# Layer 1's value projection by 512 columns: four pairs of heads in one job, with another order of filling work

## The chip, the cores and the metric

The kernel runs on one core of one Trainium2 chip. The metric is the device time of one execution in microseconds (us); lower is better. Before the change it is 1191.08 us, the median of 3 runs (1190.09 to 1192.74). One further execution was profiled: it took 1189.34 us, and its span from the first to the last instruction is 1187.6 us.

Engines are named as in the profile: PE (matrix products), PEld (its weight loads), DVE, ACT and POOL (elementwise work), and SP, whose in-order queue issues every DMA.

## The reference, cut to what matters

A trunk of two residual layers over 1024 tokens of width 1024, in float32. Layer 0 mixes a differential attention with a bidirectional linear recurrence; layer 1, which the change concerns, is a neighbourhood attention with 16 heads of 64:

```python
h = rms_norm(x, norm_g[l]) * (1.0 + scale[:, None, :]) + shift[:, None, :]
...
proj = h @ w_in                                    # (1024, 1024) @ (1024, 4096)
q, k, v, g = jnp.split(proj, 4, axis=-1)
out = neighborhood_attention(q, k, v, rpb)         # 8 x 16 window, softmax, @ v
y = (out * jax.nn.silu(g)) @ w_out
x = x + gate[:, None, :] * y
```

## The kernel before, in words

**Products in three parts.** Every large product is made of three (`mm3`, L202): both operands are split into a rounded part (`hi`) and a rest (`lo`), and hi x hi, hi x lo and lo x hi are summed in one PSUM bank. In the profile these are the lines L204, L205 and L206.

**Weights come as slabs.** The weights are cut into 80 slabs of 512 KB. `load_next` (L152) issues one slab's DMA on SP into one of two `raw` buffers. `split_next` (L161) turns it into a `hi` tile on ACT (L187) and a `lo` tile on POOL (L188); only then is the raw buffer free for the slab after next. The tiles `whi` and `wlo` have two buffers in the pool `wp`, and a third in layer 1 (`state["third"]`). `slab(i)` makes sure that slab i is split; `ahead(i)` splits it early.

**Layer 1.** The activations are split once and stay (`hact`, names `ahi` and `alo`). Of its slabs a key, query or gate slab holds 128 output columns, and `proj` (L233) multiplies it in two halves of 24 products of 512 tokens each. The value slabs go the other way round, since the attention wants tokens on the partitions: `v1_job(p)` (L1232) takes two slabs, 256 output columns, which are two pairs of heads, and for each of 8 blocks of 128 tokens it makes 24 products, with the token block as the weights and 256 columns of the slabs as the moving side. There are four such jobs (p = 0, 2, 4, 6). Each block's result is copied from PSUM into a tile `vt` (two buffers) by DVE (L1250) or ACT (L1248), in turn, and stored to DRAM (`vd`); `load_v` (L1257) reads it back in the shape that the attention wants.

**The attention** runs over 64 units (8 pairs of heads, each with 8 blocks of 128 queries) in a pipeline. `na_a(u)` makes four logit products (L667, L668), DVE adds the bias (L1351), ACT takes the exponential (L1354), and POOL normalises (L1359); `na_b(u)` transposes on PE (L1370, tiles `etr`) and copies back; `na_c` multiplies four units by the values (L1388). On PE the order is: transposes of unit u, logits of unit u + 2, some filling work, transposes of unit u + 1, and so on.

**The filling work** is layer 1's own projection, in a queue of jobs (`Feed`, L54). After each `na_a` the loop calls `feed.pump(PUMP1)`: jobs are advanced, at a price of 1300 for each step of 6 products of 512 columns or 12 of 256, until the credit of 4400 is used up (6600 for the first three units). `feed.upto(name)` runs a job to its end where the attention needs it. The first key, query and gate (slabs 40, 41, 42) are multiplied before the attention starts; the first value job's slabs are 43 and 44, and the key of pair 1 is slab 45.

**Places in SBUF.** The eight tiles `mix0` to `mix7` hold the attention's gated outputs, and are empty until these come. Slab 42 (the first gate) is already split into `mix6` and `mix7`.

**The second layer's modulation** (`mod_part`, tiles `ada`, `macc`) is accumulated on DVE, one step after each unit from unit 26 on.

A scheduler places the instructions of every engine in a fixed order; at run time each engine works through its own in that order and waits where an input is missing. SP's DMA issues wait in the same manner, so what stands behind a waiting issue waits too.

Of the kernel before, what the change touches and what calls it, by code (L numbers as in the profile page):

```python
# [11 lines left out]
F32 = mybir.dt.float32  # L12
# [7 lines left out]
P = 128  # L20
# [77 lines left out]
def kernel(ctx, tc, xT, xTp, small, lamp, adaw, tb, w0, gw, wo0, w1, nab, wo1, out):  # L98
# [62 lines left out]
    def split_next():  # L161
        i = state["split"]
        if i >= len(slabs):
            return
        while state["load"] <= i:
            load_next()
        raw = raws.pop(i)
        pool = wp
        if state["third"] is not None:
            state["turn"] = (state["turn"] + 1) % 3  # L170
            pool = wp if state["turn"] else state["third"]
        tags = ("whi", "wlo")
        if i == 2:
            pool, tags = kqp, ("ks1", "ks1")
        if i == at1["g", 0]:
            pool, tags = mixp[1], ("mix6", "mix7")
        j = i - len(slabs) + KC
        if j >= 0:

            pool = (wp, kqp, mixa, mixp[1])[j // 2]  # L180
            if j >= 2:
                tags = (("ks0", "ks0"), ("ks1", "ks1"), ("mix0", "mix1"), ("mix2", "mix3"),
                        ("mix4", "mix5"), ("mix6", "mix7"))[j - 2]
        hi = pool.tile([P, KC, P], F32R, tag=tags[0], name=f"whi{i}")
        lo = pool.tile([P, KC, P], F32R, tag=tags[1], name=f"wlo{i}")
        with tc.high_priority() if j < 2 else tc.issue_after(state["pool"]):
            A.activation(hi[:], raw[:], AF.Copy)  # L187
            G.tensor_tensor(lo[:], raw[:], hi[:], ALU.subtract)  # L188
# [260 lines left out]
    for p in range(NA_PAIRS):  # L449
        vs = [("v", p), ("v", p + 1)] if p % 2 == 0 else []  # L450
        kq = [("k", p), ("q", p)]
        order1 += kq + vs if p else kq + [("g", 0)] + vs
        if 0 < p < LATE:
            order1.append(("g", p))
    order1 += [("g", p) for p in range(LATE, NA_PAIRS)]
    base1 = {"q": 0, "k": 8, "v": 16, "g": 24}
    for key in order1:
        at1[key] = len(slabs)
# [726 lines left out]
    with tc.tile_pool(name="bound", bufs=2) as bp:  # L1185
# [36 lines left out]
    with ExitStack() as l1:  # L1222
# [9 lines left out]
        def v1_job(p):  # L1232

            i = at1["v", p]
            ws = [slab(i), slab(i + 1)]
            for t in range(8):
                hf, b = divmod(t, 4)
                ps = bank("v1")
                for k in range(KC):
                    hi, lo = (t[:, b * P:(b + 1) * P] for t in hact[k, hf])  # L1240
                    wh, wl = (w[:].rearrange("p (k a) n -> p k (a n)", a=2)[:, k % 4, :]
                              for w in ws[k // 4])
                    mm3(ps[:, :256], hi, lo, wh, wl, k == 0, k == KC - 1)
                    if k == 3:
                        yield 1300.0
                vt = ap.tile([P, 256], F32, tag="vt", name="vt", bufs=2)
                if t % 2:
                    A.activation(vt[:], ps[:, :256], AF.Copy)  # L1248
                else:
                    V.tensor_copy(vt[:], ps[:, :256])  # L1250
                state["vd"] = nc.sync.dma_start(
                    vd4[2 * hf:2 * hf + 2, 64 * b:64 * b + 64, P * p:P * p + 256], vt[:]).ins
                if t == 1:
                    ahead(i + 2)
                yield 1300.0

        def load_v(p, b):  # L1257
# [9 lines left out]

        def load_ahead(p):

            if f"1v{p + 1 - (p + 1) % 2}" in feed.done:  # L1270
                for b in range(4):
                    load_v(p + 1, b)

# [14 lines left out]

        state["gate1"] = gate1
        feed.done.add("1g0")  # L1290
        for p in range(NA_PAIRS):
            if p:
                feed.add(f"1k{p}", both(at1["k", p], evac_k(("b", p))))
                feed.add(f"1q{p}", both(at1["q", p], evac_q(("b", p))))
            if p % 2 == 0:
                feed.add(f"1v{p}", v1_job(p))
            if 0 < p < LATE:
                feed.add(f"1g{p}", both(at1["g", p], evac_g1l(p)))
        for p in range(LATE, NA_PAIRS - 2):
            feed.add(f"1g{p}", both(at1["g", p], evac_g1l(p)))  # L1300

        def last_gates():

# [101 lines left out]
        es, ets = {0: na_a(0)}, {}  # L1405
        for u in range(n_units + 1):

            pump = 1.5 * PUMP1 if u < 3 else PUMP1
            if u and u % 4 == 0:
                na_c(u - 4, [ets.pop(u - 4 + b) for b in range(4)])  # L1410
            if u % 8 == 2:

                p = u // 8
                feed.upto(f"1v{p - p % 2}")
                for b in range(4):
                    load_v(p, b)
            elif u >= 8:
# [51 lines left out]

def _slabs_v(w):  # L1470

    n = w.shape[1] // 256
    return w.reshape(2, 4, P, n, 256).transpose(3, 0, 2, 1, 4).reshape(2 * n, P, KC, P)


def _t5_bucket(rel):
# [75 lines left out]
```

## Time and profile before

| | |
|---|---|
| time, median of 3 runs | 1191.08 us (1190.09 to 1192.74) |
| time of the profiled execution | 1189.34 us |
| span of the profiled execution | 1187.6 us |
| PE busy | 1141.8 us, 96% of the span |
| DVE, ACT, POOL busy | 62%, 47%, 31% |
| products of the value jobs, 256 columns | 768 |
| chain of work that ended last | PE 74%, DVE 13%, ACT 5% |

How to read it: a matrix product's own duration in the profile holds its passage through the array, and the next product starts before it ends. What a row of products costs is therefore read from the starts in the timeline: last start less first start, divided by the number of intervals. "Granted clock" is the share of full speed that PE was given.

### The profile page before, as it was taken

How to read it: one execution, taken by the hardware profiler on the slowest of the kernel's cores; microseconds unless marked ns; L12 is line 12 of the kernel's file. 1: busy time of each engine (PE TensorE's matmuls, PEld its weight loads, DVE VectorE, ACT ScalarE, POOL GpSimd, SP SyncE). 2: the span in 40 equal slices, each digit the busy share in tenths (PEclk: the TensorE clock that was granted, in tenths of full speed). 3: DMA queues.
4: the chain of work that ended last, by engine and by line, in shares of the span. 5: the costliest groups of instructions: out<-in, count | busy, mean ns of one | idle time of the engine just before them, and what ended most of it. 6: DMA issues, size and time to landing. Idle time of an engine off the chain costs nothing.

```text
span 1187.6 us, 19215 instructions
## 1 busy us (share of the span) xinstructions
PE 1141.8 (96%) x7232; PEld 972.4 (82%) x7232; DVE 735.3 (62%) x1422; ACT 564.0 (47%) x1029; POOL 372.2 (31%) x346
## 2 busy tenths in 40 slices
PE   5999889999999999999999999999999999999997
PEld 3788768788887888777878888988998998888896
DVE  6757957689899989878663344233434443555354
ACT  4457486565655556523442444344444434445121
POOL 2124321233333322344422433332333333316100
PEclk9999999999999999999999999999999999999999
DMA  9723122423123112476513433243453534314212
GB/s 329 237 73 126 49 95 80 144 65 94 28 70 105 31 41 72 133 243 235 182 48 123 139 112 89 89 133 105 132 174 88 159 128 119 92 36 155 99 72 71
DMA packets 85789, 136.46 MB, mean 115 GB/s; under 512 B 8000, under 2 KB 49472, under 8 KB 85696
## 3 DMA queue, kind: packets, MB, share of 16 engines
q1 hardware_dynamic: 85696, 135.23, 36.7%
q8 instruction: 57, 0.93, 0.3%
q14 instruction: 36, 0.29, 0.1%
HBM read 112.13 MB, written 16.78 MB: 109 GB/s over the span
## 4 chain that ended last, share of the span: by engine, by line
PE 74%; DVE 13%; ACT 5%; DMA 3%; issue 2%; POOL 2%; SPq 0%; DVEq 0%; ACTq 0%; POOLq 0%
PE pp L204 14%; PE pp L205 14%; PE pp L206 14%; PE no L1388 4%; PE etr L1370 3%; PE v L204 2%; PE v L206 2%; PE v L205 2%; PE n L667 2%; PE atr L1003 2%; DVE e L973 2%; PE n L668 2%; POOL wlo L188 1%; PE s L667 1%; PE s L668 1%
## 5 line engine op out<-in xcount | busy, mean ns | idle before, releaser
L204 PE MATMUL pp<-ahi,whi 128*128 128x512 f32 (+1 forms) x976 | 370.2, 379 | 1.0 <-DVE sgb L673 1.0
L206 PE MATMUL pp<-ahi,wlo 128*128 128x512 f32 (+1 forms) x976 | 367.7, 377 | 1.1 <-POOL wlo L188 1.1
L205 PE MATMUL pp<-alo,whi 128*128 128x512 f32 (+1 forms) x976 | 368.1, 377 | 0.0
L188 POOL TENSOR_TENSOR wlo<-raw,whi 128x1024 fp32r<-128x1024 f32 x80 | 197.0, 2465 | 267.4 <-ACT whi L187 245.3
L206 PEld LDWEIGHTS pp<-ahi,wlo 128*128 128x128 f32 x976 | 183.8, 188 | 35.4 <-POOL wlo L188 1.6
L204 PEld LDWEIGHTS pp<-ahi,whi 128*128 128x128 f32 x976 | 183.8, 188 | 34.0 <-DVE sgb L673 1.7
L205 PEld LDWEIGHTS pp<-alo,whi 128*128 128x128 f32 x976 | 183.8, 188 | 30.4
L1359 POOL TENSOR_SCALAR e<-e,r 128x288 f32<-128x288 f32 (+1 forms) x128 | 71.1, 568 | 234.7 <-DVE r L1357 234.3
L187 ACT ACTIVATE whi<-raw 128x1024 fp32r<-128x1024 f32 x80 | 84.2, 1055 | 98.7 <-PE pp L205 52.8
L977 ACT ACTIVATE e<-e,nm 128x1024 f32<-128x1024 f32 x64 | 73.6, 1151 | 46.3 <-DVE nm L973 46.0
L1354 ACT ACTIVATE e<-e,nm 128x288 f32<-128x288 f32 (+1 forms) x128 | 72.7, 569 | 46.1 <-DVE nm L1351 39.2
L1376 DVE COPY e<-etr 96x384 f32<-96x384 f32 (+1 forms) x64 | 35.5, 554 | 95.2 <-PE etr L1370 93.5
L1351 DVE CUSTOM_DVE_ANT_0 e<-n,bias 128x288 f32<-128x288 f32 (+1 forms) x128 | 60.6, 504 | 46.8 <-PE n L668 33.0
L1374 ACT ACTIVATE e<-etr 96x384 f32<-96x384 f32 (+1 forms) x64 | 31.3, 489 | 118.3 <-DVE e L1376 118.0
L973 DVE CUSTOM_DVE_ANT_0 e<-s,tb 128x1024 f32<-128x1024 f32 x64 | 77.3, 1218 | 6.0 <-PE s L668 4.3
L994 POOL TENSOR_SCALAR e<-e,r 128x256 f32<-128x256 f32 x32 | 32.6, 1018 | 130.9 <-DVE r L983 80.7
L204 PE MATMUL v<-whi,ahi 128*128 128x256 f32 x256 | 72.2, 282 | 0.0
L206 PE MATMUL v<-whi,alo 128*128 128x256 f32 x256 | 71.9, 281 | 0.0
L205 PE MATMUL v<-wlo,ahi 128*128 128x256 f32 x256 | 71.9, 281 | 0.0
L1010 ACT ACTIVATE ath<-atr 128x512 fp32r<-128x512 f32 x64 | 37.5, 596 | 38.1 <-PE atr L1003 37.8
L1370 PE MATMUL etr<-ident,e 128*96 128x128 f32 (+1 forms) x384 | 52.5, 272 | 2.0 <-POOL e L1359 2.0
L667 PE MATMUL s<-ks,qq 128*128 128x512 f32 x128 | 52.4, 409 | 0.0
(218 smaller groups left out, 2107.7 us busy)
## 6 DMA issues: line engine op xcount, KB each, us to landing
raw<-in_w_dram SPq DMA_DIRECT2D x56, 512.0 KB
ada<-in_adaw_dram SPq DMA_DIRECT2D x96, 256.0 KB
raw<-in_wo_dram SPq DMA_DIRECT2D x24, 512.0 KB
bias<-in_nab_dram SPq DMA_DIRECT2D x64, 144.0 KB
qq<-qq SPq DMA_DIRECT2D x48, 128.0 KB
bias<-in_nab_dram SPq DMA_DIRECT2D x32, 192.0 KB
xT<-in_xT_dram SPq DMA_DIRECT2D x16, 256.0 KB
vd<-vt SPq DMA_DIRECT2D x32, 128.0 KB
```

The costliest lines, as they stand in the source:

```text
L187: A.activation(hi[:], raw[:], AF.Copy)
L188: G.tensor_tensor(lo[:], raw[:], hi[:], ALU.subtract)
L204: T.matmul(ps, lh, rh, start=start, stop=False)
L205: T.matmul(ps, lh, rl, start=False, stop=False)
L206: state["pe"] = T.matmul(ps, ll, rh, start=False, stop=stop).ins
L667: T.matmul(dst, qsel(q[m]), k, start=True, stop=False)
L973: state["dve"] = V.tensor_tensor_reduce(out=e[:], in0=ps[:].rearrange("p a b -> p (a b)"), in1=tbt["tb"][:, o:o + S], scale=-1.0, scalar=3 ...
L977: A.activation(e[:], e[:], AF.Exp, scale=-1.0, bias=nm[:], accum_out=sums[:, m:m + 1])
L1351: state["dve"] = V.tensor_tensor_reduce(out=e[:, m, :n], in0=ps[:, m, :n], in1=bias["now"][m][:, :n], scale=-1.0, scalar=3.0e38, op0=ALU.a ...
L1354: A.activation(e[:, m, :n], e[:, m, :n], AF.Exp, scale=-1.0, bias=nm[:, m:m + 1], accum_out=sums[:, m:m + 1])
L1359: state["pool"] = G.tensor_scalar(e[:, m, :n], e[:, m, :n], r[:, m:m + 1], 0.0, ALU.mult, ALU.add).ins
L1370: T.transpose(pt[:kn, m, j * P:(j + 1) * P], e[:, m, j * kn:(j + 1) * kn], ident[:])
```

## The change

One value job now makes four pairs of heads: it takes four slabs at once, and each product has 512 moving columns, so there are two jobs (p = 0 and p = 4) of 8 x 24 products in place of four of 8 x 24 products of half the width. The host lays the value slabs out accordingly: each holds two of the eight blocks of the contraction for 512 columns. The chain of 24 products starts with the third and fourth slab. The result of a token block is copied out in two halves, one by DVE and one by ACT, into the same two buffers `vt`, and stored by two DMAs.

The third and the fourth slab of a job are split into places of later outputs: `mix4`/`mix5` and `mix2`/`mix3` for the first job, `mix4`/`mix5` and `mix6`/`mix7` for the second. All four slabs of the first job are asked for before the attention starts.

The order of the jobs is written as a string. The credit is 5000 a unit up to unit 30 (twice that for unit 0, 1.5 times for units 1 and 2) and 3450 after. The modulation starts at unit 17.

```diff
-PUMP1 = 4400.0
+PUMP1 = (5000.0, 3450.0)
+JOBS1 = "k0 q0 g0 v0 k1 q1 g1 k2 q2 g2 k3 q3 v4 k4 q4 k5 q5 k6 q6 g3 k7 q7 g4 g5 g6 g7"
...
+        elif i == at1["g", 0] or i == at1["v", 4] + 3:
+            pool, tags = mixp[1], ("mix6", "mix7")
+        elif i in (at1["v", 0] + 2, at1["v", 4] + 2):
+            pool, tags = mixp[1], ("mix4", "mix5")
+        elif i == at1["v", 0] + 3:
+            pool, tags = mixa, ("mix2", "mix3")
...
-        ahead(at1["g", 0] + 2)
+        for j in range(2, 5):
+            ahead(at1["g", 0] + j)
...
-            ws = [slab(i), slab(i + 1)]
+            ws = [slab(i + j) for j in range(4)]
             for t in range(8):
                 hf, b = divmod(t, 4)
                 ps = bank("v1")
-                for k in range(KC):
+                for n, k in enumerate((4, 5, 6, 7, 0, 1, 2, 3)):
                     hi, lo = (t[:, b * P:(b + 1) * P] for t in hact[k, hf])
-                    wh, wl = (w[:].rearrange("p (k a) n -> p k (a n)", a=2)[:, k % 4, :]
-                              for w in ws[k // 4])
-                    mm3(ps[:, :256], hi, lo, wh, wl, k == 0, k == KC - 1)
-                    if k == 3:
+                    wh, wl = (w[:].rearrange("p (k a) n -> p k (a n)", a=4)[:, k % 2, :]
+                              for w in ws[k // 2])
+                    mm3(ps, hi, lo, wh, wl, n == 0, n == KC - 1)
+                    if n % 2 == 1 and n < KC - 1:
                         yield 1300.0
...
+                for j in range(2):
+                    vt = ap.tile([P, 256], F32, tag="vt", name="vt", bufs=2)
+                    src, c0 = ps[:, 256 * j:256 * j + 256], P * p + 256 * j
+                    if j:
+                        A.activation(vt[:], src, AF.Copy)
+                    else:
+                        V.tensor_copy(vt[:], src)
+                    state["vd"] = nc.sync.dma_start(
+                        vd4[2 * hf:2 * hf + 2, 64 * b:64 * b + 64, c0:c0 + 256], vt[:]).ins
...
-            pump = 1.5 * PUMP1 if u < 3 else PUMP1
+            pump = PUMP1[u > 30] * (2.0 if u == 0 else 1.5 if u < 3 else 1.0)
...
-            if u >= 26:
+            if u >= 17:
                 after_dve(mod, 1)
```

How the instructions move, at three places. First PE, where the attention of layer 1 starts, before the change: the last logits of unit 1 (`n1`), then the first value products (`v1`). The number behind `whi` and `wlo` is the slab's, the two numbers behind `ahi` and `alo` are the block of the contraction and the half of the tokens, and the last number of each name only tells tiles apart.

```order
L667 MATMUL n1_5960<-ks1_5678,qq1_5734 128x384
L668 MATMUL n1_5960<-ks1_5678,ql1_5736 128x384
L204 MATMUL v1_5976<-whi43_5885,ahi0_0_5418 128x256
L205 MATMUL v1_5976<-wlo43_5886,ahi0_0_5418 128x256
L206 MATMUL v1_5976<-whi43_5885,alo0_0_5419 128x256
L204 MATMUL v1_5976<-whi43_5885,ahi1_0_5423 128x256
```

The same place on PE after the change:

```order
L670 MATMUL n1_5972<-ks1_5678,qq1_5734 128x384
L671 MATMUL n1_5972<-ks1_5678,ql1_5736 128x384
L209 MATMUL v1_5988<-whi45_5925,ahi4_0_5514 128x512
L210 MATMUL v1_5988<-wlo45_5926,ahi4_0_5514 128x512
L211 MATMUL v1_5988<-whi45_5925,alo4_0_5515 128x512
L209 MATMUL v1_5988<-whi45_5925,ahi5_0_5519 128x512
L210 MATMUL v1_5988<-wlo45_5926,ahi5_0_5519 128x512
L211 MATMUL v1_5988<-whi45_5925,alo5_0_5520 128x512
L209 MATMUL v1_6019<-whi45_5925,ahi4_0_5514 128x512
L209 MATMUL v1_5988<-whi46_5931,ahi6_0_5562 128x512
L210 MATMUL v1_6019<-wlo45_5926,ahi4_0_5514 128x512
```

The logits stand where they stood. The first value product asked for slab 43, and now asks for slab 45; slab 46 follows 7 products later, and slabs 43 and 44 come last.

Second POOL, at the same time of the program: the splits of slabs 43 to 47 (`wlo`) and the normalising of units 0 to 2 (`e`). Before:

```order
L188 TENSOR_TENSOR wlo43_5886<-raw43_5650,whi43_5885 128x1024
L188 TENSOR_TENSOR wlo44_5920<-raw44_5706,whi44_5919 128x1024
L188 TENSOR_TENSOR wlo45_6033<-raw45_5889,whi45_6032 128x1024
L1359 TENSOR_SCALAR e_5947<-e_5947,r_5956 128x288 x2
L1359 TENSOR_SCALAR e_5963<-e_5963,r_5972 128x384 x2
L1359 TENSOR_SCALAR e_6082<-e_6082,r_6091 128x384 x2
```

After:

```order
L193 TENSOR_TENSOR wlo43_5886<-raw43_5650,whi43_5885 128x1024
L193 TENSOR_TENSOR wlo44_5920<-raw44_5706,whi44_5919 128x1024
L193 TENSOR_TENSOR wlo45_5926<-raw45_5889,whi45_5925 128x1024
L193 TENSOR_TENSOR wlo46_5932<-raw46_5923,whi46_5931 128x1024
L193 TENSOR_TENSOR wlo47_6051<-raw47_5929,whi47_6050 128x1024
L1363 TENSOR_SCALAR e_5959<-e_5959,r_5968 128x288 x2
L1363 TENSOR_SCALAR e_5975<-e_5975,r_5984 128x384 x2
L1363 TENSOR_SCALAR e_6072<-e_6072,r_6081 128x384 x2
```

The split of slab 45 keeps its place; those of 46 and 47 move ahead of unit 0.

Third SP, a little later: slab loads (`raw`), bias loads, and the stores of the value results (`vd<-vt`). Before:

```order
L158 DMA raw47_6036<-in_w1_dram 128x1024
L1327 DMA bias_5936<-in_nab_dram 128x288
L1327 DMA bias_5938<-in_nab_dram 128x288
L1327 DMA bias_5940<-in_nab_dram 128x384
L1251 DMA vd_84<-vt_6001 2x64x256
L1327 DMA bias_5942<-in_nab_dram 128x384
L1327 DMA bias_6075<-in_nab_dram 128x288
L1251 DMA vd_84<-vt_6029 2x64x256
```

After:

```order
L159 DMA raw47_5929<-in_w1_dram 128x1024
L1331 DMA bias_5948<-in_nab_dram 128x288
L1331 DMA bias_5950<-in_nab_dram 128x288
L1331 DMA bias_5952<-in_nab_dram 128x384
L159 DMA raw48_5935<-in_w1_dram 128x1024
L1331 DMA bias_5954<-in_nab_dram 128x384
L159 DMA raw49_6054<-in_w1_dram 128x1024
L1331 DMA bias_6065<-in_nab_dram 128x288
L1258 DMA vd_84<-vt_6013 2x64x256
L1258 DMA vd_84<-vt_6016 2x64x256
L1258 DMA vd_84<-vt_6044 2x64x256
```

The loads of slabs 48 and 49 now stand between the bias loads, and the stores come in pairs behind them.

More of the change, by code (lines that the diff above doesn't have):

```diff
@@ L167, in split_next @@
         raw = raws.pop(i)
-        pool = wp
-        if state["third"] is not None:
+        pool, tags = wp, ("whi", "wlo")
+        if i == 2:
+            pool, tags = kqp, ("ks1", "ks1")
+        elif i == at1["g", 0] or i == at1["v", 4] + 3:
[4 more added lines that the diff above has]
+            pool, tags = mixa, ("mix2", "mix3")
+        elif state["third"] is not None:
             state["turn"] = (state["turn"] + 1) % 3
             pool = wp if state["turn"] else state["third"]
[L172 to L176, printed above, removed]
         j = i - len(slabs) + KC
@@ L448 @@
     order1 = []
[L449 to L455, printed above, removed]
+    for key in JOBS1.split():
+        key = key[0], int(key[1])
+        order1 += [key] if key[0] != "v" else [("v", key[1] + j) for j in range(4)]
     base1 = {"q": 0, "k": 8, "v": 16, "g": 24}
@@ L1268, in load_ahead @@
         def load_ahead(p):
[L1270 removed]
+            if f"1v{p + 1 - (p + 1) % 4}" in feed.done:
                 for b in range(4):
@@ L1290 @@
         feed.done.add("1g0")
[L1291 to L1300, printed above, removed]
+        for job in JOBS1.split()[3:-2]:
+            kind, p = job[0], int(job[1])
+            evac = {"k": evac_k, "q": evac_q}.get(kind)
+            if kind == "v":
+                feed.add("1" + job, v1_job(p))
+            else:
+                feed.add("1" + job, both(at1[kind, p], evac(("b", p)) if evac else evac_g1l(p)))
         def last_gates():
```

15 lines of the change are left out of this document (4 added, 11 removed).

## The prediction

> **What bounds the kernel now.** I read the page's shares first, then a table by stage over layer 1, then who PE waited for, then PE's timeline where layer 1's attention starts. The page has PE busy for nearly the whole span, and the stretches of layer 1 tell that this is no average over different limits:
>
> ```profile
> span 1187.6 us, 19215 instructions
> PE 1141.8 (96%) x7232; PEld 972.4 (82%) x7232; DVE 735.3 (62%) x1422; ACT 564.0 (47%) x1029; POOL 372.2 (31%) x346
> ...
> 626.00:700.00 74.00, 71.28 (x507) 64.14 (x507) 24.34 (x69) 26.93 (x63) 24.05 (x28) 1.00 0.43 127
> 700.00:800.00 100.00, 100.00 (x708) 89.42 (x705) 37.62 (x111) 41.87 (x100) 35.62 (x45) 1.00 0.37 107
> 800.00:900.00 100.00, 99.86 (x732) 89.24 (x730) 43.07 (x113) 41.97 (x97) 32.61 (x39) 1.00 0.46 134
> ```
>
> The columns are the stretch, its length, and the busy time of PE, PEld, DVE, ACT and POOL, then granted clock, DMA share and GB/s. From 700 us on PE never stops, DVE and ACT are under 45%, POOL under 36%. So in layer 1 only two things can move the end: how long PE's own products take, and waits at the edges. The edge is the start, 626 to 700 us, where 2.72 us are idle:
>
> ```profile
> 628.40 0.34 PE L668 MATMUL n<-ks,ql 128*128 128x384 f32 x1
> 628.58 0.28 PE L204 MATMUL v<-whi,ahi 128*128 128x256 f32 x1
> ...
> 637.09 0.28 PE L206 MATMUL v<-whi,alo 128*128 128x256 f32 x1
> 638.84 1.01 PE L1370 MATMUL etr<-ident,e 128*96 128x128 f32 x6 [1.47 <-POOL e L1359]
> 641.10 0.44 PE L667 MATMUL n<-ks,qq 128*128 128x384 f32 x1 [1.25 <-DVE nm L1351]
> ```
>
> The first column is the start, the second the duration, and the bracket the idle time before the row and what ended it. With 72 value products done, PE stood 1.47 us for unit 0's softmax and 1.25 us for unit 1's.
>
> **The products themselves.** By their own durations the change looks large: a 256-column product lasts 282 ns, a 512-column one 391, so halving 768 to 384 would save 768 x 0.282 - 384 x 0.391 = 66 us.
>
> ```profile
> L205 PE MATMUL pp<-alo,whi 128*128 128x512 f32 x848 | 331.8, 391 | 0.0
> L204 PE MATMUL v<-whi,ahi 128*128 128x256 f32 x256 | 72.2, 282 | 0.0
> ```
>
> That is not what PE pays, since products overlap. I take starts instead. For 256 columns the stretch above gives (637.09 - 628.58) / 71 = 0.1199 us a product, and a later one of 48 products (750.27 - 744.74) / 47 = 0.1177. For 512 columns two chains of 24 give 0.2300 and 0.2265:
>
> ```profile
> 744.74 0.28 PE L204 MATMUL v<-whi,ahi 128*128 128x256 f32 x1
> ...
> 750.27 0.28 PE L206 MATMUL v<-whi,alo 128*128 128x256 f32 x1
> ```
> ```profile
> 711.99 0.39 PE L204 MATMUL pp<-ahi,whi 128*128 128x512 f32 x1
> ...
> 717.28 0.39 PE L206 MATMUL pp<-ahi,wlo 128*128 128x512 f32 x1
> ```
> ```profile
> 783.61 0.39 PE L204 MATMUL pp<-ahi,whi 128*128 128x512 f32 x1
> ...
> 788.82 0.39 PE L206 MATMUL pp<-ahi,wlo 128*128 128x512 f32 x1
> ```
>
> The first stretch belongs to the first of four jobs, so I weigh 0.1199 by one quarter and 0.1177 by three: 0.1182. Two of them are 0.2365, one wide product is 0.2283 (the mean of the two chains), and 384 x 0.0082 = **3.1 us saved**. The bounds are 384 x (2 x 0.1177 - 0.2300) = 2.0 us and 384 x (2 x 0.1199 - 0.2265) = 5.1 us. The wide form with a token block as weights isn't in this trace; the nearest row is the projection's, with the same 512 moving columns.
>
> The Trainium skill ("TensorE: Matmul & The Clock Gate", section "Wait — 56ns, not 53.3ns?") has a product cost its columns at 2.4 GHz and about 2.5 ns more whatever its size, which by its figures is an estimate of 384 x 2.5 ns = 1.0 us saved. The rows here stand some 12 ns over the columns' time at 256 and 15 at 512, so they don't bear out a fixed 2.5; the measured starts decide the sum, and the rule stands as a rival below.
>
> **The start of the attention.** The same PE rows stand up to 628.58 us. There PE now asks for slab 45, not 43. When is slab 45 there? The trace has its load, its split on ACT and its split on POOL:
>
> ```profile
> 624.14 0.33 SPq L158 DMA_DIRECT2D raw<-in_w_dram  x1
> 626.50 6.21 SPq L158 DMA_DIRECT2D raw<-in_w_dram  x2
> 632.77 1.38 SPq L1327 DMA_DIRECT2D bias<-in_nab_dram  x3
> ```
> ```profile
> 628.80 1.06 ACT L187 ACTIVATE whi<-raw 128x1024 fp32r<-128x1024 f32 x1 [3.89 <-DMA raw<-in_w_dram]
> 629.88 0.60 ACT L672 ACTIVATE sg<-pp 128x512 f32<-128x512 f32 x1
> 636.84 0.54 ACT L1354 ACTIVATE e<-e,nm 128x288 f32<-128x288 f32 x1 [6.35 <-issue]
> ```
> ```profile
> 629.94 2.42 POOL L188 TENSOR_TENSOR wlo<-raw,whi 128x1024 fp32r<-128x1024 f32 x1 [3.46 <-DMA raw<-in_w_dram]
> 638.28 0.99 POOL L1359 TENSOR_SCALAR e<-e,r 128x288 f32<-128x288 f32 x2 [5.92 <-DVE r L1357]
> ```
>
> Slab 45 is issued at 624.14, since its raw buffer is freed by the split of slab 43, and nothing ahead of it moves. A free place for its `hi` and `lo` doesn't help: ACT waited for the DMA. So `whi` is there at 629.86 and `wlo` at 632.36. The first value product waits 629.86 - 628.58 = 1.28 us; it runs 0.23; the second needs `wlo` and waits to 632.36, 2.27 us. Slab 46 then follows on POOL, 632.36 + 2.42 = 634.78; ten products bring PE there at 634.64, 0.14 us more. Together **3.7 us of new idle time**.
>
> For that the old 2.72 us go. Unit 0's transposes now stand behind 48 wide products, 632.36 + 47 x 0.228 = 643.1. What is late next: the split of slab 47, which now stands ahead of unit 0 on POOL. Its load issues once slab 45 is split, 632.4, and lands 4.7 us later if it takes as long as slab 45's (624.14 to 628.80); ACT 1.06, POOL 2.42 and unit 0's normalising 0.99 end at 641.5. That is 1.6 us under 643.1, so this wait is gone, as long as the load isn't later than that. Unit 1's bias (its DVE step ended at 641.1 before) now stands behind slab 48's load on SP, and has until 643.9. Net of the start: 3.7 - 2.7 = **1.0 us lost**.
>
> **The clock after such a gap.** Near the program's start PE was as idle once before, and the granted clock answered:
>
> ```profile
> 21.18:24.59 3.41, 1.01 (x12) 0.61 (x5) 2.24 (x4) 1.94 (x3) 1.76 (x1) 1.00 1.06 392
> 24.59:28.00 3.41, 2.89 (x7) 1.47 (x6) 3.28 (x4) 1.77 (x4) 1.05 (x1) 0.50 1.08 356
> 28.00:31.42 3.42, 3.42 (x23) 2.34 (x25) 1.54 (x3) 2.49 (x4) 0.85 (x1) 0.50 1.10 360
> 31.42:34.83 3.41, 3.41 (x77) 2.68 (x73) 1.65 (x6) 0.00 (x0) 1.51 (x1) 1.00 1.07 360
> 635.58:638.99 3.41, 1.94 (x17) 1.74 (x16) 1.65 (x7) 2.03 (x7) 0.71 (x2) 1.00 0.64 205
> 638.99:642.41 3.42, 2.17 (x15) 1.72 (x15) 1.12 (x5) 0.71 (x2) 0.60 (x2) 1.00 0.16 54
> ```
>
> After a stretch with 1.01 of 3.41 us busy the clock was 0.50 for two such stretches. Around the present gaps of 1.47 and 1.25 us, 1.94 and 2.17 us were busy and it stayed at 1.00. The new gap leaves a single product in 628.58 to 632.36, under 0.4 of 3.8 us, well below the stretch that cost the clock. So I take it that the clock halves. One stretch at half costs 3.41 / 2 = **1.7 us**, two cost 3.4. I take one, since PE is full from 632.4 on, while 24.59 to 28.00 was busy for 2.89 of 3.41; two stay in the range. The skill (same page, "What's actually happening") has the clock halve after an idle window of about 3.4 us and return after one busy window; the trace agrees with the length, 3.41, and not with the return, which took two.
>
> **The other edits cost nothing, each under a cover.** The copies of the value results and their stores are as many as before (32 of 256 columns). The modulation is moved, not changed; DVE is at 43% where it goes. The lower credit after unit 30 puts 12 or 18 products between transposes. A unit's softmax has then 30 products, transposes and logits, 30 x 0.228 + 1.3 = 8.1 us, and needs 3.2, from the last logit's end at 1053.41 to POOL's at 1056.59:
>
> ```profile
> 1053.12 0.29 PE L668 MATMUL n<-ks,ql 128*128 128x288 f32 x1
> ```
> ```profile
> 1055.60 0.99 POOL L1359 TENSOR_SCALAR e<-e,r 128x288 f32<-128x288 f32 x2 [4.31 <-DVE r L1357]
> ```
>
> The second job's slabs are asked for when POOL is a third busy. If one of these covers failed, each would cost what it exceeds.
>
> **The sum.** -3.1 + 1.0 + 1.7 = -0.4 us on the profiled execution's 1189.34 us, so 1188.9. That execution is 1.74 us under the median of the runs, 1191.08, so the forecast for the median is 1190.7, and its own range, with the bounds of the products and of the clock, is 1188.7 (5.1 saved) to 1193.5 (2.0 saved, two stretches at half). A measurement can tell about 0.2%, 2.4 us, from no change; this is inside it.
>
> **Rivals.** (1) *The clock holds*, because the one product between the two waits, or where the 3.41 us stretches happen to be cut, keeps it up. Then -3.1 + 1.0 = -2.1 us, and with the upper bound of the products -4.1: 1189.0 to 1187.0. At the very end the last unit's transposes wait for a softmax that the new order gives the same 24 products, in two pieces; should that wait go too, it is 0.50 more, 1186.5:
>
> ```profile
> 1080.94 0.53 PE L1370 MATMUL etr<-ident,e 128*96 128x128 f32 x3 [0.50 <-POOL e L1359]
> ```
>
> For it: no gap in layer 1 has cost the clock so far. Against: the busy share is far under the one that did.
>
> (2) *Stores take the place of the waits: slower.* A chain of the second job fills both `vt` buffers, so the next chain's two copies wait for both stores. Stores stand on SP behind bias loads, which wait for DVE:
>
> ```profile
> SPq L1327 <- DVE nm L1351: 126.2, 39, 15.3
> ...
> 647.97 0.42 DVE L1250 COPY vt<-v 128x256 f32<-128x256 f32 x1 [2.90 <-DMA vd<-vt]
> ```
>
> The longest such wait was 15.3 us, and once a copy already held DVE for 2.90. ACT and DVE work in order, so a held copy holds the softmax behind it. The cover is two chains with transposes and logits less the softmax, 2 x 5.5 + 1.3 - 3.2 = 9.1 us; from there on PE stands. One hold of 15.3 costs 6.2 us: -0.4 + 6.2 = +5.8, 1196.9. Against: such long waits fall where SP has nothing else that is due.
>
> (3) *A wide product saves less than the rows say*, a fixed small sum for each product left out, 1.0 us in all: 1.0 + 1.7 - 1.0 = +1.7, and with two stretches at half +3.4: 1192.8 to 1194.5. Against: all four pairings of the rows give 2.0 or more. This is the rule of the page named above.
>
> That the change isn't made as told has no chance of its own: the new order shows products of 512 columns.
>
> **How the numbers follow.** Forecast 0.42: 0.34 of it within 0.2%, 0.04 on each side. Clock holds 0.33: 0.27 faster, 0.06 within. Stores 0.13, all slower. Small saving 0.12: half within, half slower. That makes faster 0.31, same 0.46, slower 0.23. The range reaches from rival 1's far end to rival 3's, 1186.5 to 1194.5, and leaves out rival 2.
>
> **What would show it.** In the profile after: first value product at 629.9 and the second at 632.4, with waits for `whi` and `wlo` that sum to 3.7 us; a granted clock of 0.50 for one or two stretches right after; no wait of the first transposes; starts of the value products 0.228 apart. The forecast is wrong if these starts are 0.224 or less, if PE stands at the second job or among the last units, or if the first gap is absent.

## The result: slower, where no measurable change was forecast

| | before | after |
|---|---|---|
| median, us | 1191.14 (6 runs, 1189.53 to 1192.74) | 1199.81 (6 runs, 1197.54 to 1203.89) |
| profiled execution, us | 1189.34 | 1198.46 |
| its span, us; mean granted clock | 1187.6; 0.995 | 1196.7; 0.989 |

The ratio is 1.0067, with a 95% interval of 1.0047 to 1.0087. The changed kernel was run once more beside the later experiments and gave 1.0075 (1.0047 to 1.0102). The forecast was 1190.7, in a range up to 1194.5.

The changed kernel's table by stage follows, with the columns of the prediction's table (stretch, its length, busy time of PE, PEld, DVE, ACT and POOL, granted clock, DMA share, GB/s):

```profile
span 1196.7 us, 18445 instructions
PE 1146.5 (96%) x6848; PEld 957.5 (80%) x6848; DVE 734.3 (61%) x1422; ACT 564.3 (47%) x1029; POOL 372.9 (31%) x346
```
```profile
626.00:700.00 74.00, 69.75 (x350) 57.47 (x350) 15.18 (x43) 19.94 (x43) 20.53 (x18) 0.98 0.40 121
628.30:631.70 3.40, 1.01 (x3) 0.66 (x4) 0.69 (x1) 2.05 (x3) 2.67 (x2) 1.00 0.14 53
631.70:635.10 3.40, 3.40 (x9) 2.60 (x9) 0.08 (x1) 0.60 (x1) 2.05 (x1) 0.51 0.86 287
696.60:700.00 3.40, 2.16 (x20) 1.62 (x17) 1.83 (x3) 0.49 (x1) 0.83 (x1) 1.00 0.39 129
700.00:703.40 3.40, 3.40 (x10) 2.62 (x10) 1.21 (x6) 1.30 (x4) 0.86 (x2) 0.51 0.06 25
1085.80:1089.20 3.40, 0.08 (x3) 0.05 (x1) 3.40 (x4) 0.01 (x1) 2.28 (x1) 1.00 0.56 165
1089.20:1092.60 3.40, 3.40 (x15) 2.54 (x16) 1.15 (x2) 2.02 (x3) 1.90 (x1) 0.50 0.42 143
1092.60:1096.00 3.40, 3.40 (x9) 2.65 (x8) 1.70 (x2) 1.58 (x2) 2.58 (x4) 0.50 0.55 178
```

The share of PE is 96% in both kernels and tells nothing. The stretches do: there are three places where PE stands, and behind each the clock is at one half, for 3.4, 3.4 and 6.8 us. PE's timeline has the rows that waited, with the idle time in brackets:

```profile
628.75 0.50 PE L209 MATMUL v<-whi,ahi 128*128 128x512 f32 x1 [1.08 <-ACT whi L192]
631.18 0.50 PE L210 MATMUL v<-wlo,ahi 128*128 128x512 f32 x1 [1.94 <-POOL wlo L193]
...
672.19 0.39 PE L209 MATMUL v<-whi,ahi 128*128 128x512 f32 x1
...
678.09 0.39 PE L211 MATMUL v<-whi,alo 128*128 128x512 f32 x1
...
697.83 1.45 PE L1392 MATMUL no<-e,vc 96*64 96x128 f32 x12 [1.09 <-DVE e L1380]
...
788.67 0.87 PE L1392 MATMUL no<-e,vc 96*64 96x128 f32 x10 [0.92 <-ACT e L1378]
...
1089.15 2.12 PE L1392 MATMUL no<-e,vc 96*64 96x128 f32 x12 [3.32 <-DVE e L1380]
```

The first place was forecast: 3.0 us of waiting for `whi` and `wlo` and one stretch at half clock. The products came out as forecast too: in this stretch 26 steps from 672.19 to 678.09 are 0.2269 us each, so two 256-column products (0.2365 in the prediction's weighing) became one of 0.2269, 384 x 0.0096 = 3.7 us in all (3.1 forecast). The other two places were not forecast. Both are products of attention weights with values (`no`) that wait for a copy of transposes on DVE (L1380): one at the first block of layer 1, one at the last. The fourth wait in the rows, 0.92 us at 788, is for the same kind of copy on ACT (L1378), which stood there behind two slab splits and two copies of keys from 785.01 to 788.10; no clock fell behind it, and no run tried to take it out.

| term, us | forecast | profiled executions |
|---|---|---|
| products | -3.1 | -3.1 to -3.7 |
| start: new idle less old | +1.0 | 3.0 - 2.7 = +0.3 |
| start: clock at half, one stretch | +1.7 | +1.7 |
| first attention block: idle, clock | 0 | 1.09 + 1.7 |
| block at 788 | 0 | +0.9 |
| last block: idle less the old 0.50, two stretches of clock | 0 | 2.8 + 3.4 |
| sum | -0.4 | +8.2 to +8.8, of +9.12 measured |

**Why the last block waits.** DVE's timeline of the changed kernel at that place, and POOL's:

```profile
1078.80 1.29 DVE L234 TENSOR_TENSOR alo<-sg,ahi 128x512 fp32r<-128x512 f32 x2
...
1080.42 0.56 DVE L1380 COPY e<-etr 128x384 f32<-128x384 f32 x1
1080.90 0.77 DVE L234 TENSOR_TENSOR alo<-sg,ahi 128x512 fp32r<-128x512 f32 x1
1081.59 7.04 DVE L234 TENSOR_TENSOR alo<-o,ahi 128x512 fp32r<-128x512 f32 x4
1088.55 0.54 DVE L1380 COPY e<-etr 96x384 f32<-96x384 f32 x1
```
```profile
1082.53 5.55 POOL L193 TENSOR_TENSOR wlo<-raw,whi 128x1024 fp32r<-128x1024 f32 x2
```

Unit 63's transposes began on PE at 1082.89 and took 0.82. On DVE five splits of the output projection's input (L234, which makes `alo`) stood between the copy of unit 62's transposes and theirs, and the last four took 7.04 us where four of 0.69 take 2.8. These ran beside two slab splits on POOL. In the kernel before, six such splits were through before POOL's slab splits began, and both copies followed:

```profile
1076.61 1.28 DVE L229 TENSOR_TENSOR alo<-sg,ahi 128x512 fp32r<-128x512 f32 x2
...
1077.89 0.66 DVE L229 TENSOR_TENSOR alo<-sg,ahi 128x512 fp32r<-128x512 f32 x1
1078.48 2.11 DVE L229 TENSOR_TENSOR alo<-o,ahi 128x512 fp32r<-128x512 f32 x3
1080.51 0.55 DVE L1376 COPY e<-etr 128x384 f32<-128x384 f32 x1
1081.58 0.55 DVE L1376 COPY e<-etr 96x384 f32<-96x384 f32 x1 [0.52 <-PE etr L1370]
```
```profile
1080.93 5.21 POOL L188 TENSOR_TENSOR wlo<-raw,whi 128x1024 fp32r<-128x1024 f32 x2
```

There, 24 products stood between the last logits and unit 62's transposes, so six splits ran ahead of unit 62's copy. The lower credit cuts the 24 into 12 before these transposes and 12 behind them. Unit 62's copy then went ahead of all but two of the splits, and the rest moved into POOL's time.

**Why the first block waits.** SyncE's queue and DVE of the changed kernel:

```profile
682.76 0.49 SPq L1258 DMA_DIRECT2D vd<-vt  x1
683.35 4.60 SPq L1272 DMA_DIRECT2D vc<-vd  x4
688.05 1.37 SPq L1331 DMA_DIRECT2D bias<-in_nab_dram  x2
```
```profile
692.60 0.46 DVE L1355 CUSTOM_DVE_ANT_0 e<-n,bias 128x288 f32<-128x288 f32 x1 [3.51 <-DMA bias<-in_nab_dram]
...
697.22 0.55 DVE L1380 COPY e<-etr 96x384 f32<-96x384 f32 x1
```

The value loads (L1272) held the queue for 4.60 us, since they read what the last store (L1258) had yet to write. Unit 4's second bias stood behind them. DVE waited 3.51 us for it, and unit 3's copy, which the last 12 `no` of this block need, stood behind that on DVE.

The last store itself was late. The job's last product began at 678.09, but the two `vt` buffers were still being stored:

```profile
679.18 0.42 DVE L1257 COPY vt<-v 128x256 f32<-128x256 f32 x1 [5.01 <-DMA vd<-vt]
```

ACT's last copy, which feeds the last store, began only at 682.36. Over the whole kernel the copies of value results waited 65.7 us for stores (17 waits; 8.1 us in 4 before the change), and PE never for them.

### The profile page after: what moved, and what is told of

Read it like the earlier page. It is cut to its first block, busy times and chain, and to the rows that moved or that the text cites. A ratio compares the mean times of both kernels' runs of the same rounds, so it can differ in the third digit from the quotient of the medians.

```text
span 1196.7 us, 18445 instructions
## 1 busy us (share of the span) xinstructions
PE 1146.5 (96%) x6848; PEld 957.5 (80%) x6848; DVE 734.3 (61%) x1422; ACT 564.3 (47%) x1029; POOL 372.9 (31%) x346
## 4 chain that ended last, share of the span: by engine, by line
PE 74%; DVE 13%; ACT 5%; DMA 3%; issue 3%; POOL 1%; SPq 0%; DVEq 0%; ACTq 0%; POOLq 0%
PE pp L209 14%; PE pp L210 14%; PE pp L211 14%; PE no L1392 3%; PE etr L1374 3%; PE v L210 2%; PE v L209 2%; PE v L211 2%; PE atr L1006 2%; PE n L670 2%; DVE e L976 2%; PE n L671 2%; PE s L670 1%; PE s L671 1%; POOL wlo L193 1%
## 5 line engine op out<-in xcount | busy, mean ns | idle before, releaser
L1380 DVE COPY e<-etr 96x384 f32<-96x384 f32 (+1 forms) x64 | 35.5, 554 | 80.3 <-PE etr L1374 78.4
L1378 ACT ACTIVATE e<-etr 96x384 f32<-96x384 f32 (+1 forms) x64 | 31.3, 488 | 103.3 <-DVE e L1380 99.0
L1127 ACT ACTIVATE sq<-xh 128x512 f32<-128x512 f32 (+1 forms) x37 | 19.9, 538 | 75.2 <-DVE xh L1122 75.2
L1122 DVE SCALAR_TENSOR_TENSOR xh<-pp,mod,xh 128x512 f32<-128x512 f32 (+1 forms) x37 | 23.4, 633 | 51.4 <-PE pp L211 50.2
L1392 PE MATMUL no<-e,vc 96*64 96x128 f32 (+1 forms) x768 | 49.0, 278 | 5.6 <-DVE e L1380 4.4
L210 PE MATMUL v<-wlo,ahi 128*128 128x512 f32 x128 | 50.6, 395 | 1.9 <-POOL wlo L193 1.9
```

What stands on the lines that cost most here:

```text
L210: T.matmul(ps, lh, rl, start=False, stop=False)
L1392: T.matmul(po[64 * m:64 * m + 64, b * P:(b + 1) * P], vch[p, b][:kn, j + hf, 64 * m:64 * m + 64], ets[b][:kn, m, j * P:(j + 1) * P], start ...
```

## The experiments

In the expectations VectorE is DVE, ScalarE is ACT, GpSimd is POOL and SyncE is SP. The theory: the loss is these separate gaps; the two at the first and the last block are made by what stands ahead of a copy on DVE, and the clock that falls behind them adds to each. The rival: the wide products with their four slabs, or the new order as a whole, cost a little everywhere, and the gaps are only where it shows. Ratios are to the kernel before on the same chip, with 95% intervals; 0.0010 of ratio is 1.2 us. The runs were spread over several chips, so ratios are compared, not times.

**The splits behind the last copy**

```diff
-                    V.tensor_copy(e[:kn, m, :], pt[:kn, m, :384])
+                    state["etr"] = V.tensor_copy(e[:kn, m, :], pt[:kn, m, :384]).ins
...
+                    with tc.issue_after(state["etr"]) if l and hf else nullcontext():
-                    split_act(k, hf, ...)
+                        split_act(k, hf, ...)
```

> The changed kernel, with VectorE's splits of the output projection's second half of tokens put behind the copy of the last unit's transposes on VectorE; nothing else moves. Theory (three gaps in PE's row, each followed by a clock at half): the 3.3 us gap before the last block of layer 1's attention goes, and with it the two stretches at half clock (3.4 us): 1198.5 - 6.7 = 1191.8 in the profiled execution, at least 3.3 us less (1195.2) where the clock falls all the same. Rival (the wide value products or their order cost a little everywhere, and the gap is only where the delay shows): the same wait comes back elsewhere and the time stays at 1197 or more.

Measured: 1188.21 in the profiled execution, median 1192.85 (12 runs), ratio 1.0014 (0.9998 to 1.0031). By ratios the one edit gives back 0.0053, 6.3 us. The profiled execution lies 3.6 us under the 1191.8 that was expected: in it the clock didn't fall at the first block (1.7 us), and PE waited 2.5 us at the start in place of 3.0. DVE and PE at the last block:

```profile
1080.56 0.55 DVE L1381 COPY e<-etr 96x384 f32<-96x384 f32 x1 [2.85 <-PE etr L1375]
```
```profile
1079.64 0.82 PE L1375 MATMUL etr<-ident,e 128*96 128x128 f32 x6
1080.39 2.84 PE L1393 MATMUL no<-e,vc 96*64 96x128 f32 x48
```

Now DVE waits for PE, and the 48 `no` products stand in one row without a bracket. The clock stays at 1.00 there. The theory holds: no wait of PE took the gap's place in layer 1. The splits are still slow beside POOL (the next three take 3.46 us), but nothing waits for them.

**The same edit on the kernel before**, whose lines are the same but for their numbers

> The kernel before, with the same edit of the splits (behind the last copy on VectorE). Theory: nothing to win there, since both last copies stand ahead of the splits already and the only wait at the end is 0.50 us for GpSimd: 1191.4, within 0.1%. Rival (putting the splits behind the copy is worth 6 us in any kernel, whatever the order of the filling work): 1185.

Measured: 0.9988 (0.9969 to 1.0007). So the edit is no general gain; it mends what the new order broke.

**POOL's two slab splits left out**

```diff
-            G.tensor_tensor(lo[:], raw[:], hi[:], ALU.subtract)
+            if i in (73, 74):
+                A.activation(lo[:], raw[:], AF.Copy)
+            else:
+                G.tensor_tensor(lo[:], raw[:], hi[:], ALU.subtract)
```

ACT writes a plain copy of the raw slab in place of the difference, so this kernel leaves the low halves of two slabs out of the computation.

> The changed kernel, but the low halves of slabs 73 and 74 (output projection) are not computed on GpSimd as a difference: ScalarE writes a plain copy of the raw slab in their place, so part of the split is left out of the computation; the order on VectorE stays with the last copy behind five splits. Theory (the splits on VectorE took 2.8 us instead of 0.69 since GpSimd ran its slab splits at the same time): each takes about 0.69, the four rows 2.8 instead of 7.04, the last copy comes 4.2 us earlier, the 3.3 us gap is under 0.5, and the clock holds: 1198.5 - 2.8 to 6.7 = 1191.8 to 1195.7. Rival (the splits are slow for another reason, or the order alone makes the gap): the rows stay near 7 us, the gap at 3 us, the time at 1198.

Measured: ratio 1.0010 (0.9992 to 1.0028), median 1194.43, and 1189.89 in the profiled execution, below the expected 1191.8 to 1195.7; here too the clock didn't fall at the first block. DVE, with the same order as in the changed kernel:

```profile
1079.55 2.71 DVE L237 TENSOR_TENSOR alo<-o,ahi 128x512 fp32r<-128x512 f32 x4
1082.19 0.54 DVE L1383 COPY e<-etr 96x384 f32<-96x384 f32 x1
```

The four splits take 2.71 us instead of 7.04, and PE has no wait at the last block. So the order alone wasn't enough to make the gap in the changed kernel: it took the order and POOL's work at the same time. The Trainium skill ("SBUF — State Buffer", section "SBUF: two separate sides") says that a VectorE operation with two SBUF inputs and a GpSimd operation that reads SBUF take turns at a shared pair of ports, the one that comes second being blocked for the whole of the other. The rows agree: of the eight L234 between 1078 and 1095 us in the changed kernel, six took 0.68 to 0.91 us. The two that started inside a slab split took 2.82 and 2.86, and each ended 0.55 us after that slab split did; a slab split took 5.55 / 2 = 2.78 there. The kernel before has a pair of the same kind, at a place where PE didn't wait:

```profile
1088.29 2.48 DVE L229 TENSOR_TENSOR alo<-o,ahi 128x512 fp32r<-128x512 f32 x1 [1.59 <-ACT ahi L228]
```
```profile
1087.82 2.40 POOL L188 TENSOR_TENSOR wlo<-raw,whi 128x1024 fp32r<-128x1024 f32 x1 [0.48 <-ACT whi L187]
```

**The value loads behind the bias**

```diff
                 feed.upto(f"1v{p - p % 4}")
+                es[u + 1] = na_a(u + 1)
...
-        with tc.issue_after(state["vd"]):
+        with tc.issue_after(state["vd"]), tc.issue_after(state["bias"]):
```

> The changed kernel, with the four loads of values of units 2 and 34 put behind the next unit's bias loads on SyncE's queue. Theory: the second bias of unit 4 was issued at 688.4, behind value loads that waited 4.6 us for the last store; now it is issued by about 683.5, VectorE is not held from 689.0 to 692.6, the copy of unit 3's transposes comes in time, and the gap of 1.09 us with its stretch at half clock (1.7 us) goes: 1198.5 - 2.8 = 1195.7. Rival (the gap comes from the copies of values that wait for their stores, 5 us each, which stay): the gap stays at about 1 us and the time at 1198.5.

Measured: 1195.00 profiled, median 1195.61, ratio 1.0043 (1.0026 to 1.0061), 2.9 us better than the changed kernel. SyncE's queue has the bias ahead now:

```profile
684.02 0.49 SPq L1258 DMA_DIRECT2D vd<-vt  x1
684.61 0.81 SPq L1331 DMA_DIRECT2D bias<-in_nab_dram  x1
685.47 4.51 SPq L1272 DMA_DIRECT2D vc<-vd  x4
```

DVE waits 1.74 us for it in place of 3.51, and PE doesn't wait at the first block. So the order on SyncE's queue is what made this gap. Its size is known less well: the intervals of this kernel and of the changed one overlap at their ends, and moving the modulation alone (further down) gave the same 1.0043. The gap is also unsteady: in five profiles without this edit it was 1.09, 0.97, 0.68, 0.52 and 0.40 us, and only the first was followed by half clock.

**The value chains from chunk 0**

```diff
-                for n, k in enumerate((4, 5, 6, 7, 0, 1, 2, 3)):
+                for n, k in enumerate(range(KC)):
```

> The changed kernel, with the value chains taking the chunks in the order 0 to 7, so that they begin with the first two slabs, which are there at once. Theory: the first value products wait only for the third slab, after 12 products (628.6 + 2.7 = 631.3 against 632.4 for its low half), and for the fourth (634.8): some 2 us idle instead of 3.0, but spread, so the share of busy time stays above one half and the stretch at half clock (1.7 us) goes: 1198.5 - 0.9 - 1.7 = 1195.9; the gaps later on stay. Rival (the start is not a cost, since layer 1 has slack): 1198.5.

Measured: slower than the changed kernel, 1.0102 (1.0085 to 1.0120); 1202.19 profiled where 1195.9 was expected. The expectation failed in its sum, not at its place. At the start the waits are 0.20 and 1.84 us and the clock holds, as expected. But later SyncE and DVE show:

```profile
681.95 2.70 SPq L159 DMA_DIRECT2D raw<-in_w_dram  x2
684.74 1.08 SPq L1258 DMA_DIRECT2D vd<-vt  x2
685.87 6.34 SPq L1272 DMA_DIRECT2D vc<-vd  x4
692.31 1.64 SPq L1331 DMA_DIRECT2D bias<-in_nab_dram  x2
```
```profile
697.28 0.46 DVE L1355 CUSTOM_DVE_ANT_0 e<-n,bias 128x288 f32<-128x288 f32 x1 [7.84 <-DMA bias<-in_nab_dram]
```

Two slab loads now stand ahead of the last two stores, the value loads wait 6.34 us, DVE 7.84, and PE 5.3 at the first block, with two stretches at half clock. It is the mechanism of the first block's gap, with a longer hold.

**All three edits at once**: splits, value loads and chunk order

> The changed kernel with both edits and the value chains in the order 0 to 7. By itself that order cost time, since two loads of slabs then stood ahead of the last stores on SyncE, and the value loads and the bias behind them came later (gap of 5.3 us before the first attention block instead of 1.1). Theory: with the bias ahead of the value loads that gap goes, and what the order takes at the start (1.0 us idle, 1.7 us of clock) is a gain: 1183.5 to 1186. Rival (the stores, which come later in any case, hold the first attention block through its value loads): a gap of 2 us or more stays there, and the time is at or above that of the two edits alone.

Measured: 0.9992 (0.9972 to 1.0012), 1194.06 profiled. The rival held: a gap of 2.26 us stays at the first block, as the stores themselves come later.

**Both mends: splits and value loads**

> The changed kernel with both edits: the splits behind the last copy, and the value loads behind the next unit's bias loads. Theory (the gaps are separate losses): 1188.2 of the first edit alone less what the second took by itself in its profile's middle (1.09 idle, up to 1.7 of clock): 1185.4 to 1187.1, faster than the kernel before by 0.2 to 0.3%. Rival (a delay taken out in one place comes back at the next): 1188 or more.

Measured: 0.9972 (0.9956 to 0.9987), median 1189.75 (12 runs), profiled 1189.05. It is faster than the kernel before, by 0.28%, and 0.0095 under the changed kernel, where the single edits gave 0.0053 and 0.0024, which add up within their intervals. The profiled execution lies 2 us over what was expected and in the rival's range. The gap at the first block is gone there, but PE's waits in layer 1 sum to 4.4 us, against 4.3 with the first edit alone: the start has 3.4 us in place of 2.5, and the block at 786 has 1.06 in place of 0.78. So the rows don't show the 0.0042 (5 us) that the ratios give the second edit on top of the first. The mean granted clock over all executions, 0.992 here and 0.990 there, goes the same way; what makes it stays open.

**The order alone, with products of 256 columns**

The kernel before with the new order (each value job of four pairs written as two jobs of two), the new credits and the earlier modulation; and the same with both mends:

```diff
-PUMP1 = 4400.0
+PUMP1 = (5000.0, 3450.0)
+JOBS1 = "k0 q0 g0 v0 v2 k1 q1 g1 k2 q2 g2 k3 q3 v4 v6 k4 q4 k5 q5 k6 q6 g3 k7 q7 g4 g5 g6 g7"
...
-            pump = 1.5 * PUMP1 if u < 3 else PUMP1
+            pump = PUMP1[u > 30] * (2.0 if u == 0 else 1.5 if u < 3 else 1.0)
...
-            if u >= 26:
+            if u >= 17:
```

> The kernel before, with the changed kernel's order of filling work, credits and earlier modulation, but value products of 256 columns as before (two pairs of heads a job, two jobs one behind the other). Theory: VectorE's order at the end is that of the changed kernel (the last copy stands behind five splits), so the end costs 3.3 - 0.5 us of idle and up to 3.4 us of clock here too: 1189.3 + 6.2 = 1195.5, and between 1192 and 1197 by how the clock falls; the gap of 3.0 us at the first value product, which asks for the third slab first, is absent. Rival (the width, with its four slabs, is what costs): 1189 to 1191 and no gap at the end.

> The kernel before with the changed kernel's order, credits and earlier modulation and with both edits, but value products of 256 columns. Against the two edits on the changed kernel (1189.8) it tells what the width is worth. Theory: the products cost 3.1 us more, PE's waits for the copies of values (4.6 us in the profile of the order alone) stay, and the start has less to wait for (about 2): 1194 to 1198; by the ratios of the single edits 1205.9 - 6.3 - 2.9 = 1196.7. Rival (the width is worth nothing, and the order alone makes all of the difference): 1189 to 1191.

Measured: 1.0122 (1.0102 to 1.0141) and 1.0095 (1.0072 to 1.0119), both slower than expected. The end's gap is there at 256 columns too, 2.12 us, so the width doesn't make it. What the expectation had too small is what else waits: PE's list of waits for the order alone, in layer 1 (total, times, longest, in us):

```profile
PE no L1382 <- DVE e L1370: 4.9, 2, 2.8
PE v L205 <- DVE vt L1247: 3.3, 2, 2.4
PE v L206 <- POOL wlo L189: 1.4, 1, 1.4
PE v L205 <- ACT vt L1245: 1.3, 1, 1.3
```

With narrow products the value chains on PE wait for copies of results, which wait for stores. In the changed kernel PE has no such wait. Against the two mends (0.9972), the pairs with the same mends stand 0.0123 higher: in this order the wide job is worth about 15 us, several times the 3.7 of its products. That is the job as a whole, with its four slabs, their places and the copies in halves; the number of columns by itself wasn't tested. Of the 15, the products, the waits for copies (3.2 and 1.4 in that profile) and a gap of 2.8 us at the first block with two stretches at half clock make up most; the rest wasn't traced.

**Keys 1 ahead of the first value job**

On top of both mends:

```diff
-JOBS1 = "k0 q0 g0 v0 k1 q1 g1 ..."
+JOBS1 = "k0 q0 g0 k1 v0 q1 g1 ..."
```

> The changed kernel with the two edits, and keys 1 in the order of filling work ahead of the first value job. Theory (the start's idle time comes from slabs that are not there yet, and 48 products ahead of them hide it): the waits at the first value products, 3.3 us in the profile of the two edits, go, and with them any half clock there; the time is 2.5 to 5 us under the two edits' 1189.8: 1185 to 1187.3. Rival (the value job now ends later, so its stores, the value loads and the first attention block come late): a gap of over 1 us before the first attention block and no gain.

Measured: 1.0162 (1.0141 to 1.0184), slower by far than expected. The waits at the start are down to 0.9 us, but the filling work is out of step with the units: transposes of later units wait 8.1 us in all, and the last three units have none of it left. The layer's last block comes at 1108.7 us instead of 1083.8. Not all of this was followed.

**The old credits**

```diff
-PUMP1 = (5000.0, 3450.0)
+PUMP1 = (4400.0, 4400.0)
...
-            pump = PUMP1[u > 30] * (2.0 if u == 0 else 1.5 if u < 3 else 1.0)
+            pump = PUMP1[u > 30] * (1.5 if u < 3 else 1.0)
```

> The changed kernel with the credits of before (4400 a unit throughout, 1.5 times that for the first three). Theory (the lower credit is not the loss: it keeps filling work for the last units, and only the place of the last copy was missed): the filling work is used up by unit 58, so five or six units have nothing between logits and transposes and PE stands for most of a softmax of 3.2 us in each, 10 to 20 us, more with the clock at half: 1205 to 1220. Rival (the lower credit splits the last 24 products and so makes the gap): 1192 to 1195.

Measured: 1.0198 (1.0176 to 1.0221), median 1215.82, in the theory's range. From 1085 to 1107 us PE's timeline has three filling products for the last seven units. The waits that the profile lists there sum to 2.5 us only, and others fall earlier (2.0 us at 1005), so the whole of the loss wasn't followed. The new order needs a lower credit; what went wrong is where it put the last 24 products.

**The modulation from unit 26**

```diff
-            if u >= 17:
+            if u >= 26:
```

> The changed kernel with the modulation of layer 1's output begun at unit 26 again, as before. Theory (the modulation hides under products, and none of the three gaps comes from it): the same as the changed kernel, 1.0067 of the kernel before within 0.0020, with the gaps of 1.1 us at the first attention block and 3.3 us at the last. Rival (the earlier modulation's loads on SyncE and steps on VectorE are what makes copies and splits late): 1192 to 1195.

Measured: 1.0043 (1.0026 to 1.0060), under the theory's 1.0047 to 1.0087 and over the rival's times. Its gap at the first block was 0.52 us without half clock, and the gap at the last block was there, 3.30 us with two stretches. To settle it, the changed kernel was run again, and the mended version with unit 26:

> The changed kernel once more, as it is, beside the next one. Theory (the modulation costs nothing, and the gap at the first attention block is just at the point where the clock falls in some executions and not in others): 1.0050 to 1.0065 of the kernel before, between the two results so far, with executions of 1196 to 1203 us. Rival (the earlier modulation costs 2 to 3 us): 1.0067 or more.

> The version with both edits (splits behind the last copy, value loads behind the bias) and the modulation begun at unit 26 again. Theory (the modulation costs nothing): 0.9972 of the kernel before within 0.0015, as with both edits alone. Rival (the earlier modulation costs 2 to 3 us): 0.9950 or less.

Measured: 1.0075 (1.0047 to 1.0102) and 0.9994 (0.9975 to 1.0013). Both expectations missed, in opposite ways: the first number is the rival's, the second lies over the theory's. In the mended version the earlier modulation costs nothing that shows. Why the unmended kernel came out lower without it stays open; the order of SyncE's queue around the first block is the same in both. And 0.9994 for the nearest version leaves the 0.28% of the two mends less sure than its interval says.

## Why the prediction was wrong, point by point

- *Products*: right. 0.2269 us a product where 0.2283 was forecast. These starts refute rival 3, the small saving.
- *Start*: the mechanism right, 3.0 us idle instead of 3.7. Slab 45 was split 1.1 to 1.2 us earlier than forecast and PE came 0.9 us earlier, and the third wait, for slab 46, was absent, since the products before it ran at half clock.
- *Clock*: right at the start in this execution, one stretch, and in seven of the nine profiles with this start. The step was applied to one gap; four such stretches were paid in this execution. The reason given for one and not two, that PE is full in the first of them, held behind the first two gaps and not behind the last: there the clock stayed down for two stretches with PE busy for 3.40 of 3.40 us in the first.
- *"The other edits cost nothing, each under a cover"*: this failed, and it is the step that made the forecast wrong: a term put at 0 was 2.8 us of idle time and 3.4 us of clock, 6.2 of the 9.1 measured. For the lower credit the cover was worked out against a softmax of 3.2 us, and that cover held: no transposes wait for POOL at the end. But behind the transposes stands a copy on DVE, and the prediction never asked what DVE does between. The order of DVE's instructions had the copy behind the splits; the rows of before had most splits at 0.69 us and POOL's at 2.6. Priced apart, the splits fit; side by side they don't, and the row at 1088.29 of the kernel before (2.48 us) already showed it. Putting the splits behind the copy or taking POOL's two away removes the gap: 0.0053 and 0.0057 of ratio, 6 to 7 us.
- *Rival 2, stores on SyncE's queue*: the right queue with the wrong order. Its first half came true, in the first job: copies waited some 5 us for stores, and PE had cover for that. But what then held PE was not stores behind bias loads, with a hold of 15.3 us. It was a bias behind value loads behind the late last store, with 4.60 us and then 1.09 on PE and one stretch of clock. The sum had this at 0 as well.
- *"The forecast is wrong if ... PE stands at the second job or among the last units"*: it stood among the last units (3.32 us), and that point showed the error. It also stood once near the second job, 0.92 us at 788.

## What to carry to other kernels

When an edit changes how much work fills the gap ahead of a step, follow the step to its last consumer, and on each engine of that chain read what stands ahead in the queue and what runs beside it on an engine that slows it (here POOL's slab splits beside DVE's splits). A short gap costs more than itself when the clock falls behind it, and all three gaps that did this here lay at an edge of the layer's attention, so that is the first place to search. And a wider product can be worth more through the copies and stores behind it than by what it saves on PE.

## What the runs showed of the hardware

- DVE's `tensor_tensor` of 128x512 took 0.69 us alone and up to 2.86 us beside POOL's `tensor_tensor` of 128x1024, which took 2.78 there instead of 2.4.
- PE's busy share of a stretch doesn't tell by itself whether the clock falls. A stretch with 2.16 of 3.40 us busy was followed by half clock; in the kernel before, one with 1.94 of 3.41 was not. The stretches are cut where the clock's own steps lie: in the changed kernel its falls stand at 631.8, 700.1 and 1089.2, which are 20 and 114 times 3.413 us apart. The Trainium skill ("TensorE: Matmul & The Clock Gate", section "What's actually happening") gives one idle window of about 3.4 us as the condition; here a window that was idle for 36% was followed by it.
- The scatter of one kernel's times goes with its mean granted clock: 35 runs of the kernel before on one chip were from 1187.91 us at 0.995 to 1197.58 at 0.985. Single executions therefore can't tell a gap of 1 us; their rows can.
